# Strassen's seven block products for three and four pairs of k tiles in two down projections

## The chip, the cores and the metric

One core of one Trainium2 chip runs the whole kernel. The metric is device time in microseconds of one execution; shown are the median and the range of three runs. One further execution was profiled, and every row below is from it.

## The reference, cut to what matters

```
def swiglu(x, w_gate, w_up, w_down):
    return (jax.nn.silu(x @ w_gate) * (x @ w_up)) @ w_down
...
        x = layer_norm(alpha * x + 0.5 * swiglu(x, ffn_w_gate[l, 0], ffn_w_up[l, 0], ffn_w_down[l, 0]),
                       ln_g[l, 0], ln_b[l, 0])
        x = layer_norm(alpha * x + hybrid_mixer(x, w_in[l], b_gate[l], diff_lambda[l], diff_subln_g[l],
                                                w_br_moba[l], w_br_diff[l], w_br_sb[l], w_out[l], l),
                       ln_g[l, 1], ln_b[l, 1])
        x = layer_norm(alpha * x + 0.5 * swiglu(x, ffn_w_gate[l, 1], ffn_w_up[l, 1], ffn_w_down[l, 1]),
                       ln_g[l, 2], ln_b[l, 2])
```

There is one layer, 256 tokens, a model width of 1024 and a feed-forward width of 2816. The change lies in the two products with `ffn_w_down`: hidden values of 256 x 2816 times a weight of 2816 x 1024.

## The kernel before

All operands are float32. Each is split into a high part in TensorE's float32r format and the remainder in the same format, and a product is made of three matmuls: high by high, high by low, low by high (`nat_mm`). The hidden values stand transposed in `hT`: per k tile of 128 hidden columns, 256 columns of high parts and 256 of low parts. `xT` holds the transposed input of the gate and up products in the same way.

**Weights.** `Weights` brings every weight as a chunk of 128 x 1024 (or 128 x 768). SyncE issues its transfer into a tile `raw` (5 buffers), ScalarE writes the high half of a tile `w` (9 buffers) or `wx` (3 more, where memory is free), VectorE subtracts and writes the low half. `pump` does this ahead of use as far as buffers allow: with 12 buffers, chunk c is split once chunk c - 12 is used up. So a split's place on ScalarE's and VectorE's queues is where `W.done()` stands in the code. All engines run in order; the program's order is the code's order, except for jobs that `pe.later` puts at a planned TensorE time.

**A feed-forward block.** `ffn` makes 22 hidden tiles (j = 0 to 21) with `trn_mms` and `evac`, and then calls `down`. `down` has 22 k tiles. For all but the last 6 (the tail) it takes one chunk and runs 12 matmuls of 512 columns: two token tiles t, two halves hf of the 1024 columns, three matmuls each, into four PSUM banks `acc`. Then it takes the 6 chunks of the tail and finishes one bank after another: t = 0 hf = 0, t = 0 hf = 1, then t = 1. After each bank `residual` adds it to ALPHA times `x` and makes statistics; `normalise` does the layer norm; `turn_tile`, planned 5.9 us later on TensorE's own count (`T_X`), transposes the normalised `x` with TensorE into `xT`, which the next stage reads. In the first block that next stage is the value projection (`vals`, chunks of 768); the second block ends the kernel.

`down` is also called for the output projection of the mixer, where nothing changes.

Of the kernel before, what the change touches and what calls it, by code (L numbers as in the profile page):

```python
# [21 lines left out]
NF = FF // P  # L22
# [4 lines left out]
ALPHA = 2.0 ** 0.25  # L27
# [3 lines left out]


HL_BUFS = 9
RAW_BUFS = 5
START = 4
WARM = 7

NAT = 2

TAIL_FF, IN_FF = 6, 2  # L40
# [20 lines left out]
class Weights:  # L61
# [34 lines left out]
    def split(self):  # L96
        i = self.n_split
        if i >= self.n_dma:
            self.load()
        _, n, scale = self.chunks[i]  # L100
        raw = self.raw.pop(i)
        w = self.tile(i)
        h, l = w[:, 0, :], w[:, 1, :]
        hv = h.bitcast(F32)
        if scale is None:
            self.nc.scalar.activation(h[:, :n], raw[:, :n], AF.Copy)  # L106
            self.nc.vector.tensor_tensor(l[:, :n], raw[:, :n], hv[:, :n], op=ALU.subtract)  # L107
        else:
            self.nc.scalar.activation(h[:, :n], raw[:, :n], AF.Copy, scale=scale)
            self.nc.vector.scalar_tensor_tensor(  # L110
                l[:, :n], raw[:, :n], scale, hv[:, :n], op0=ALU.mult, op1=ALU.subtract)
        self.hl[i] = (h, l)
        self.n_split += 1

    def pump(self):

# [74 lines left out]
def trunk(ctx: ExitStack, tc: tile.TileContext, start_d, x_d, ln_g, ln_b, gu_d, gun_d, down_d, v_d, qk_d, gate_d,  # L191
# [17 lines left out]
    for f in range(2):  # L209
        nat = NAT if f else 0  # L210
        for b in range(nat):
            chunks += [(gun_d[b, i], 1024, None) for i in range(4)]
        for j in range(2, NF) if f == 0 else range(2 * nat, NF):
            chunks += [(gu_d[f, j, i], 1024, None) for i in range(2)]
        chunks += [(down_d[f, k * P:(k + 1) * P, :], 1024, None) for k in range(NF)]
# [19 lines left out]
    def act_split(dst_h, dst_l, src):  # L235
        nc.scalar.activation(dst_h, src, AF.Copy)  # L236
        nc.vector.tensor_tensor(dst_l, src, dst_h.bitcast(F32), op=ALU.subtract)
# [100 lines left out]
        nc.gpsimd.dma_start(out=b, in_=ln_b[i].partition_broadcast(P))  # L338
        ln_par[i] = (g, b)

    def residual(t, lo, n, ps, st):
        xs = x[:, t, lo:lo + n]
        nc.vector.scalar_tensor_tensor(xs, xs, ALPHA, ps[:, 0:n], op0=ALU.mult, op1=ALU.add)  # L343
        nc.vector.bn_stats(st, xs)

    def normalise(i, t, st, last):
# [60 lines left out]
    def down(lhs, nk, tail, inline, i, last=False):  # L407


        banks = [[acc.tile([P, 512], F32, name="acc") for _ in range(2)] for _ in range(2)]  # L410
        for k in range(nk - tail):
            (h, l), = W.take(1)
            for t in range(2):
                for hf in range(2):
                    nat_mm(banks[t][hf], lhs, k, t, h, l, hf * 512, 512, k == 0,
                           last and t == 1 and hf == 1 and k == nk - tail - 1)
            W.done()
        ws = W.take(tail)

        def part(t, hf, n):  # L420
            k = nk - tail + n
            h, l = ws[n]
            nat_mm(banks[t][hf], lhs, k, t, h, l, hf * 512, 512, k == 0, n == tail - 1)

        for t in range(2):
            st = small.tile([P, 3, 6], F32, name="st")
            left = tail
            if t == 0 or last:
                for n in range(tail):
                    part(t, 0, n)  # L430
                residual(t, 0, 512, banks[t][0], st[:, 0, :])
            if t == 0:
                for n in range(tail):
                    part(t, 1, n)
                residual(t, 512, 512, banks[t][1], st[:, 1, :])
            elif last:
                xs = x[:, t, 512:]
                nc.vector.scalar_tensor_tensor(xs, xs, ALPHA, banks[t][1], op0=ALU.mult, op1=ALU.add)
                for c in range(2):
                    ps = acc.tile([P, 512], F32, name="acc")  # L440
                    for n, (h, l) in enumerate(ws):
                        nat_mm(ps, lhs, nk - tail + n, t, h, l, 512 + c * S, S, n == 0, n == tail - 1)
                    xs = x[:, t, 512 + c * S:512 + (c + 1) * S]
                    nc.vector.tensor_tensor(xs, xs, ps[:, 0:S], op=ALU.add)  # L444
                    nc.vector.bn_stats(st[:, 1 + c, :], xs)  # L445
            else:
                for n in range(tail):
                    part(1, 0, n)
                    part(1, 1, n)
                    if n < inline:  # L450
                        W.done()
                        left -= 1
                for hf in range(2):
                    residual(t, hf * 512, 512, banks[t][hf], st[:, hf, :])
            normalise(i, t, st[:, 0:3 if last and t else 2, :], last)
        if last:
            W.done(left)
        else:
            pe.later(DONE_AT, lambda: W.done(left))


    def ffn(f, i):
        with ExitStack() as es:
            hp = es.enter_context(tc.tile_pool(name="hp", bufs=1))
            tmp = es.enter_context(tc.tile_pool(name="ftmp", bufs=3))
            hT = hp.tile([P, NF, 2 * S], F32R, name="hT")

            def evac(j, banks, free):
                res = []
                for ps in banks:  # L470
                    lo = tmp.tile([P, S], F32, name="lo")
                    nc.scalar.activation(lo, ps[:, S:2 * S], AF.Copy)  # L472
                    v = tmp.tile([P, S], F32, name="gu")
                    nc.vector.tensor_tensor(v, ps[:, 0:S], lo, op=ALU.add)  # L474
                    res.append(v)
                g, u = res
                W.done(free)
                nc.scalar.activation(g, g, AF.Silu)
                nc.vector.scalar_tensor_tensor(u, u, 0.5, g, op0=ALU.mult, op1=ALU.mult)  # L479
                W.done(free)  # L480
                act_split(hT[:, j, 0:S], hT[:, j, S:2 * S], u)

            if f == 0:

                banks = [att.tile([P, 512], F32, name="att") for _ in range(2)]
                for k in range(KT):
                    w, c = first[k // 2], slice((k % 2) * 512, (k % 2) * 512 + 512)
                    for x_lo, w_lo in ((0, 0), (1, 0), (0, 1)):
                        for t in range(2):
                            a = xT[:, k, x_lo * S + t * P:x_lo * S + (t + 1) * P]  # L490
                            pe.mm(banks[t], a, w[:, w_lo, c], k == 0 and x_lo + w_lo == 0, k == KT - 1 and w_lo == 1)
                    if k % 2:
                        W.free(W.held.pop(-k), True)
                units = []
                for t in range(2):
                    pv = banks[t].rearrange("p (j g c) -> p g j c", j=2, g=2)
                    units.append(hidden(tmp, t, pv[:, 0], pv[:, 1]))
                pe.later(N_T, lambda: turn_hidden(hT, 0, units))
            else:
                nat_gate_up(tmp, hT, NAT)  # L500
            for j in range(2 if f == 0 else 2 * NAT, NF):
                ws = W.take(2)
# [5 lines left out]
            down(hT, NF, TAIL_FF, IN_FF, i, last=f == 1)  # L508

    def nat_gate_up(tmp, hT, nat):  # L510
        ws = W.take(4 * nat)
# [459 lines left out]
```

## Time and profile before

| | |
|---|---|
| median of 3 runs | 599.26 us (599.05 to 599.38) |
| the profiled execution's own time | 599.37 us |
| its span, first to last instruction | 597.7 us |
| TensorE busy | 587.9 us |
| VectorE busy | 407.5 us |
| ScalarE busy | 327.0 us |

The span is what the profile shows; the 1.7 us between it and that execution's time lie around it. A busy TensorE is one with a matmul under way, not one at its peak.

### The profile page before, as it was taken

The page shows a single profiled execution, that of the slowest core. Times are in us where ns is not written, and L with a number is a line of the kernel's source. Part 1 is how long each engine was busy: PE and PEld are TensorE (multiplying, and loading weights), DVE is VectorE, ACT ScalarE, POOL GpSimd, SP SyncE. Part 2 cuts the span into 40 slices and gives each one's busy share as a digit, 9 for nine tenths or more (in the row PEclk, how much of TensorE's full clock was granted, in tenths as well). Part 3 has the DMA queues.
Part 4 walks back from the last instruction along what each step waited for, and adds up shares of the span by engine and source line. Part 5 has one row for each costly group of instructions (what it writes and reads, how often), then busy time and mean ns, then how long its engine had stood idle before and what let it go on. Part 6 is the DMA issues. An engine that isn't in the chain of part 4 may idle for free.

```text
span 597.7 us, 8548 instructions
## 1 busy us (share of the span) xinstructions
PE 587.9 (98%) x3150; PEld 505.4 (85%) x3150; DVE 407.5 (68%) x655; ACT 327.0 (55%) x550; POOL 36.2 (6%) x77
## 2 busy tenths in 40 slices
PE   8999999999999999999999999999999999999994
PEld 7888888888888998888888878888898898888884
DVE  6889777674338746597977685889867766764216
ACT  5878656663312758596657654644665665654100
POOL 0610000000001003110001000001000000000002
PEclk9999999999999999999999999999999999999998
DMA  8998755666442676354547447356965566564001
GB/s 308 326 392 303 255 183 180 206 185 227 140 127 63 209 249 239 115 176 149 171 141 243 144 163 255 107 172 225 316 240 180 178 205 184 181 214 165 1 0 70
DMA packets 32537, 113.34 MB, mean 190 GB/s; under 512 B 3680, under 2 KB 4448, under 8 KB 32496
## 3 DMA queue, kind: packets, MB, share of 16 engines
q1 hardware_dynamic: 30816, 106.97, 53.9%
q0 software_dynamic: 1680, 5.83, 2.9%
q8 instruction: 24, 0.39, 0.3%
q14 instruction: 17, 0.14, 0.1%
HBM read 111.74 MB, written 1.05 MB: 189 GB/s over the span
## 4 chain that ended last, share of the span: by engine, by line
PE 98%; DMA 1%; DVE 0%; POOLq 0%; SPq 0%; POOL 0%; ACT 0%; issue 0%; DVEq 0%
PE acc L182 91%; PE att L182 5%; PE att L186 2%; DMA sraw<-start 1%; DVE x L361 0%; POOLq L965 0%; SPq L246 0%; POOL rs L351 0%; ACT w L272 0%; DVE st L445 0%; DVE x L444 0%; DVEq L965 0%; DVE mv L350 0%
## 5 line engine op out<-in xcount | busy, mean ns | idle before, releaser
L107 DVE TENSOR_TENSOR w<-raw,w 128x1024 fp32r<-128x1024 f32 (+1 forms) x166 | 197.7, 1207 | 62.4 <-ACT w L106 61.8
L182 PE MATMUL acc<-xT,w 128*128 128x512 f32 (+1 forms) x1264 | 226.4, 337 | 0.0
L182 PEld LDWEIGHTS acc<-xT,w 128*128 128x128 f32 x1264 | 196.2, 190 | 26.7 <-issue 1.0
L106 ACT ACTIVATE w<-raw 128x1024 fp32r<-128x1024 f32 (+1 forms) x166 | 170.2, 1041 | 68.9 <-PE acc L182 60.3
L182 PE MATMUL acc<-w,xT 128*128 128x512 f32 (+1 forms) x576 | 128.2, 379 | 0.0
L182 PEld LDWEIGHTS acc<-w,xT 128*128 128x128 f32 x576 | 105.5, 188 | 18.6 <-issue 1.0
L182 PE MATMUL acc<-w,hT 128*128 128x512 f32 (+1 forms) x408 | 93.1, 383 | 0.0
L182 PEld LDWEIGHTS acc<-w,hT 128*128 128x128 f32 x408 | 75.2, 188 | 15.0
L472 ACT ACTIVATE lo<-acc 128x256 f32<-128x256 f32 x76 | 28.7, 383 | 57.5 <-PE acc L182 57.5
L474 DVE TENSOR_TENSOR gu<-acc,lo 128x256 f32<-128x256 f32 x76 | 31.5, 422 | 34.8 <-ACT lo L472 34.6
L182 PE MATMUL acc<-xT,wx 128*128 128x256 f32 (+1 forms) x240 | 46.1, 337 | 0.0
L107 DVE TENSOR_TENSOR wx<-raw,wx 128x1024 fp32r<-128x1024 f32 (+1 forms) x30 | 36.3, 1213 | 13.2 <-ACT wx L106 13.0
L182 PEld LDWEIGHTS acc<-xT,wx 128*128 128x128 f32 x240 | 37.5, 190 | 4.4
L106 ACT ACTIVATE wx<-raw 128x1024 fp32r<-128x1024 f32 (+1 forms) x30 | 31.3, 1047 | 12.1 <-PE acc L182 10.2
L182 PE MATMUL acc<-wx,hT 128*128 128x512 f32 (+1 forms) x138 | 32.8, 380 | 0.0
L182 PEld LDWEIGHTS acc<-wx,hT 128*128 128x128 f32 x138 | 25.2, 188 | 4.9
L351 POOL TENSOR_SCALAR rs<-mv 128x1 f32<-128x1 f32 x6 | 4.7, 778 | 405.4 <-DVE mv L350 405.4
L343 DVE SCALAR_TENSOR_TENSOR x<-x,acc 128x512 f32<-128x512 f32 x11 | 7.5, 682 | 27.2 <-PE acc L182 27.2
L182 PE MATMUL acc<-w,oT 128*128 128x512 f32 x108 | 25.7, 393 | 0.0
L182 PEld LDWEIGHTS acc<-w,oT 128*128 128x128 f32 x108 | 20.1, 188 | 4.4 <-issue 0.3
L236 ACT ACTIVATE hT<-gu 128x256 fp32r<-128x256 f32 x38 | 15.8, 415 | 11.6 <-DVE gu L479 11.6
L479 DVE SCALAR_TENSOR_TENSOR gu<-gu 128x256 f32<-128x256 f32 x38 | 15.9, 419 | 0.0
(146 smaller groups left out, 401.3 us busy)
## 6 DMA issues: line engine op xcount, KB each, us to landing
raw<-gu SPq DMA_DIRECT2D x76, 512.0 KB, 4.8
raw<-down SPq DMA_DIRECT2D x44, 512.0 KB, 4.1
raw<-gates SPq DMA_DIRECT2D x24, 512.0 KB, 4.4
raw<-qk SPq DMA_DIRECT2D x18, 512.0 KB, 4.6
raw<-v SPq DMA_DIRECT2D x12, 384.0 KB, 3.1
raw<-w_out SPq DMA_DIRECT2D x8, 512.0 KB, 4.4
raw<-gun SPq DMA_DIRECT2D x8, 512.0 KB, 4.3
sraw<-start SPq DMA_DIRECT2D x7, 384.0 KB, 6.3
```

The costliest lines, as they stand in the source:

```text
L106: self.nc.scalar.activation(h[:, :n], raw[:, :n], AF.Copy)
L107: self.nc.vector.tensor_tensor(l[:, :n], raw[:, :n], hv[:, :n], op=ALU.subtract)
L182: self.nc.tensor.matmul(out, lhsT=lhsT, rhs=rhs, start=start, stop=stop, **kw)
L186: self.nc.tensor.transpose(out, in_, ident)
L236: nc.scalar.activation(dst_h, src, AF.Copy)
L343: nc.vector.scalar_tensor_tensor(xs, xs, ALPHA, ps[:, 0:n], op0=ALU.mult, op1=ALU.add)
L351: nc.gpsimd.tensor_scalar(rs, mv[:, 1:2], EPS, None, op0=ALU.add)
L472: nc.scalar.activation(lo, ps[:, S:2 * S], AF.Copy)
L474: nc.vector.tensor_tensor(v, ps[:, 0:S], lo, op=ALU.add)
L479: nc.vector.scalar_tensor_tensor(u, u, 0.5, g, op0=ALU.mult, op1=ALU.mult)
```

## The change

For the k tiles just ahead of the tail, two k tiles ka and kb are taken together: 3 pairs in the first feed-forward block, 4 in the second. Over a pair the product is a 2 x 2 by 2 x 2 product of blocks: rows are the token tiles t, columns the halves hf, the inner index ka and kb. Instead of 8 block products (24 matmuls of 512 columns) it makes 7 (21 matmuls) by Strassen's algorithm in Winograd's form.

Four operands are sums of hidden blocks (`sums_T`, at the head of `down` for all pairs; written to `xT`, which is free by then, after a high/low split). Four are sums of weight blocks: a pair's weights become four chunks named "first" to "fourth", made by `split_sums` from the two `raw` tiles. Four products go to PSUM banks of their own (`p1`, `p5`, `p6`, `p7`, pool `att`), three straight into `acc`. After the last pair, ScalarE copies `p1` and eight VectorE instructions add the four banks to `x`, with a scratch tile `u`. `residual` then scales by 1.0. The tile `sums` has one buffer that `sums_T`, "third", "fourth" and `u` share; `raw` goes from 5 buffers to 4.

```diff
-RAW_BUFS = 5
+RAW_BUFS = 4
...
+PAIRS = (3, 4)
...
+    def split_cols(self, src, h, l, cs):
+        self.nc.scalar.activation(h[:, cs], src, AF.Copy)
+        self.nc.vector.tensor_tensor(l[:, cs], src, h[:, cs].bitcast(F32), op=ALU.subtract)
+
+    def split_sums(self, which, raw, h, l):
...
+        sub, lo, hi = self.nc.vector.tensor_tensor, slice(0, 512), slice(512, 1024)
+        if which == "first":
+            self.upper = raw
+            self.split_cols(raw[:, lo], h, l, lo)
+            sub(raw[:, lo], raw[:, hi], raw[:, lo], op=ALU.subtract)
+            self.split_cols(raw[:, lo], h, l, hi)
+        elif which == "third":
+            self.sums = self.raw_pool.tile([P, 1024], F32, name="sums", bufs=1)
+            sub(self.sums.rearrange("p (i c) -> p i c", i=2),
+                self.lower[:, hi].unsqueeze(1).to_broadcast([P, 2, 512]),
+                self.upper.rearrange("p (i c) -> p i c", i=2), op=ALU.subtract)
+            self.split_cols(self.sums, h, l, slice(0, 1024))
+        else:
+            sub(self.lower[:, lo], self.lower[:, lo], self.sums[:, lo], op=ALU.subtract)
+            self.split_cols(self.lower[:, lo], h, l, lo)
...
+    def sums_T(lhs, ka, kb, i):
...
+        t = rawp.tile([P, 1024], F32, name="sums", bufs=1)
+        tt = nc.vector.tensor_tensor
+        for n, k in enumerate((ka, kb)):
+            hl = lhs[:, k, :].bitcast(F32)
+            tt(t[:, n * S:(n + 1) * S], hl[:, 0:S], hl[:, S:2 * S], op=ALU.add)
+        a, c, b, d, s1, s2, s3, s4 = (t[:, n * P:(n + 1) * P] for n in range(8))
+        tt(s1, c, d, op=ALU.add)
+        tt(s2, s1, a, op=ALU.subtract)
+        tt(s3, a, c, op=ALU.subtract)
+        tt(s4, b, s2, op=ALU.subtract)
+        place = xT[:, 2 * i:2 * i + 2, :].rearrange("p k (n c) -> p (k n) c", c=2 * P)
+        act_split(place[:, :, 0:P], place[:, :, P:2 * P], t[:, 512:1024].rearrange("p (n c) -> p n c", c=P))
+        return [(place[:, n, 0:P], place[:, n, P:2 * P]) for n in range(4)]
...
+        std = nk - tail - 2 * pairs
+        s_ops = [sums_T(lhs, std + 2 * n, std + 2 * n + 1, n) for n in range(pairs)]
+        for k in range(std):
...
+                for m, prods in enumerate((((p1, plain(ka, 0)), (p5, s1)),
+                                           ((banks[0][0], plain(kb, 0)), (banks[0][1], s4)),
+                                           ((p6, s2), (p7, s3)),
+                                           ((banks[1][0], plain(kb, 1)),))):
+                    for half, (ps, (a, al)) in enumerate(prods):
...
+                        pe.mm(ps, a, h, first, False)
+                        pe.mm(ps, a, l, False, False)
+                        pe.mm(ps, al, h, False, end)
+                    W.done()
+            u = rawp.tile([P, 1024], F32, name="sums", bufs=1)[:, 0:512]
...
+            nc.scalar.activation(u, p1, AF.Copy)
+            add(0, 0, p1, ALPHA)
+            nc.vector.tensor_tensor(u, u, p6, op=ALU.add)
+            add(0, 1, u, ALPHA)
+            add(0, 1, p5, 1.0)
+            nc.vector.tensor_tensor(u, u, p7, op=ALU.add)
+            add(1, 0, u, ALPHA)
+            add(1, 1, u, ALPHA)
+            add(1, 1, p5, 1.0)
         ws = W.take(tail)
```

What this does to VectorE's order is seen at two places. The first is the start of the first `down`, from the end of hidden tile 21 on (L237 before and L278 after write `hT`; L107 before and L116 after are the plain split of a chunk). Before:

```order
L107 TENSOR_TENSOR w<-raw,w 128x1024
L237 TENSOR_TENSOR hT<-gu,hT 128x256
L107 TENSOR_TENSOR w<-raw,w 128x1024 x3
L107 TENSOR_TENSOR wx<-raw,wx 128x1024
L107 TENSOR_TENSOR w<-raw,w 128x1024 x2
```

After, the operands of the first pair (L455 to L460 are the sums of `sums_T`, the last row is their split):

```order
L116 TENSOR_TENSOR w<-raw,w 128x1024
L278 TENSOR_TENSOR hT<-gu,hT 128x256
L455 TENSOR_TENSOR sums<-hT 128x256 x2
L457 TENSOR_TENSOR sums<-sums 128x128
L458 TENSOR_TENSOR sums<-sums 128x128
L459 TENSOR_TENSOR sums<-sums 128x128
L460 TENSOR_TENSOR sums<-sums 128x128
L278 TENSOR_TENSOR xT<-sums,xT 128x4x128
```

The last six of these rows follow twice more, for the other pairs, and then come the weights. The rows down to the first L126 of 512 columns are "third" and "fourth" of the first pair, whose "first" and "second" stand before the sums; then come the second pair's four chunks (L126 is a low half in `split_cols`; L136, L140 and L145 are the weight sums of "first", "third" and "fourth"):

```order
L140 TENSOR_TENSOR sums<-raw 128x1024
L126 TENSOR_TENSOR w<-sums,w 128x1024
L145 TENSOR_TENSOR raw<-raw,sums 128x512
L126 TENSOR_TENSOR w<-raw,w 128x512 x2
L136 TENSOR_TENSOR raw<-raw 128x512
L126 TENSOR_TENSOR w<-raw,w 128x512
L116 TENSOR_TENSOR wx<-raw,wx 128x1024
L140 TENSOR_TENSOR sums<-raw 128x1024
L126 TENSOR_TENSOR w<-sums,w 128x1024
L145 TENSOR_TENSOR raw<-raw,sums 128x512
L126 TENSOR_TENSOR w<-raw,w 128x512
```

Where two splits stood for two k tiles, eight VectorE instructions stand per pair, and five of them read what a ScalarE instruction has just written. The second place is the end of the first `down`'s splits (768 columns are chunks of the value projection). Before:

```order
L107 TENSOR_TENSOR w<-raw,w 128x768 x5
L107 TENSOR_TENSOR wx<-raw,wx 128x768
L343 SCALAR_TENSOR_TENSOR x<-x,acc 128x512
L344 BN_STATS st<-x 128x6
L343 SCALAR_TENSOR_TENSOR x<-x,acc 128x512
```

After:

```order
L116 TENSOR_TENSOR w<-raw,w 128x768 x2
L116 TENSOR_TENSOR wx<-raw,wx 128x768
L505 SCALAR_TENSOR_TENSOR x<-x,att 128x512
L509 TENSOR_TENSOR sums<-sums,att 128x512
L505 SCALAR_TENSOR_TENSOR x<-x,sums 128x512
L505 SCALAR_TENSOR_TENSOR x<-x,att 128x512
L512 TENSOR_TENSOR sums<-sums,att 128x512
L505 SCALAR_TENSOR_TENSOR x<-x,sums 128x512 x2
L505 SCALAR_TENSOR_TENSOR x<-x,att 128x512
L384 SCALAR_TENSOR_TENSOR x<-x,acc 128x512
L385 BN_STATS st<-x 128x6
```

The eight additions of the product banks stand between the splits and the first residual, and the splits of six value chunks stand ahead of them.

## Rows read from the trace of the kernel before

**Rows 1.** The page: busy time by engine, and the chain that ended last.

```profile
PE 587.9 (98%) x3150; PEld 505.4 (85%) x3150; DVE 407.5 (68%) x655; ACT 327.0 (55%) x550; POOL 36.2 (6%) x77
...
PE 98%; DMA 1%; DVE 0%; POOLq 0%; SPq 0%; POOL 0%; ACT 0%; issue 0%; DVEq 0%
```

**Rows 2.** Stretches: us; busy PE, PEld, DVE, ACT, POOL; clock; DMA.

```profile
128.20:155.40 27.20, 27.20 (x122) 22.52 (x121) 14.46 (x14) 12.44 (x14) 0.00 (x0) 1.00 0.63 199
...
551.40:573.10 21.70, 21.70 (x97) 17.98 (x96) 3.67 (x3) 3.18 (x3) 0.00 (x0) 1.00 0.00 1
```

**Rows 3.** Timeline of PE, first down: start, length, line, tiles, count.

```profile
128.16 8.32 PE L182 MATMUL acc<-w,hT 128*128 128x512 f32 x36
136.32 2.88 PE L182 MATMUL acc<-wx,hT 128*128 128x512 f32 x12
...
186.19 1.03 PE L186 MATMUL att<-ident,x 128*128 128x128 f32 x8
...
188.90 3.31 PE L182 MATMUL acc<-w,xT 128*128 128x384 f32 x18
```

**Rows 4.** Timeline of DVE, first down; in brackets the idle time before and its releaser.

```profile
130.93 0.42 DVE L479 SCALAR_TENSOR_TENSOR gu<-gu 128x256 f32<-128x256 f32 x1
131.26 1.22 DVE L107 TENSOR_TENSOR w<-raw,w 128x1024 fp32r<-128x1024 f32 x1
132.40 0.42 DVE L237 TENSOR_TENSOR hT<-gu,hT 128x256 fp32r<-128x256 f32 x1
...
134.89 1.23 DVE L107 TENSOR_TENSOR w<-raw,w 128x1024 fp32r<-128x1024 f32 x1 [0.89 <-ACT w L106]
...
175.96 0.69 DVE L343 SCALAR_TENSOR_TENSOR x<-x,acc 128x512 f32<-128x512 f32 x1 [2.24 <-PE acc L182]
176.69 0.69 DVE L344 BATCH_NORM_STATS2 st<-x 128x6 f32<-128x512 f32 x1
...
181.49 0.21 DVE L350 BATCH_NORM_AGGREGATE mv<-st 128x2 f32<-128x12 f32 x1
...
184.71 0.75 DVE L361 SCALAR_TENSOR_TENSOR x<-x,rs,ln_b 128x512 f32<-128x512 f32 x1
```

**Rows 5.** Timeline of ACT, first down.

```profile
133.80 1.06 ACT L106 ACTIVATE w<-raw 128x1024 fp32r<-128x1024 f32 x1 [1.05 <-PE acc L182]
```

**Rows 6.** Groups of DVE and ACT by form: count, busy us, mean ns, idle before.

```profile
L889 DVE TENSOR_TENSOR G<-G 128x512 f32<-128x512 f32 x8 | 5.5, 692 | 0.3
L710 DVE TENSOR_TENSOR o<-att,rsm 128x256 f32<-128x256 f32 x3 | 1.3, 425 | 1.0 <-PE att L182 1.0
L613 DVE CUSTOM_DVE_ANT_0 e<-att,base 128x128 f32<-128x128 f32 x12 | 3.4, 287 | 0.0
...
L236 ACT ACTIVATE w<-sraw 128x512 fp32r<-128x512 f32 x5 | 3.1, 616 | 0.0
```

**Rows 7.** Timeline of PE, second down: its start and its last matmuls.

```profile
529.60 13.76 PE L182 MATMUL acc<-w,hT 128*128 128x512 f32 x60
...
588.59 1.24 PE L182 MATMUL acc<-w,hT 128*128 128x256 f32 x9
```

**Rows 8.** Timeline of DVE, second down.

```profile
533.84 0.42 DVE L237 TENSOR_TENSOR hT<-gu,hT 128x256 fp32r<-128x256 f32 x1
...
577.40 0.69 DVE L343 SCALAR_TENSOR_TENSOR x<-x,acc 128x512 f32<-128x512 f32 x1 [18.03 <-PE acc L182]
...
590.79 0.24 DVE L350 BATCH_NORM_AGGREGATE mv<-st 128x2 f32<-128x18 f32 x1
```

**Rows 9.** The same view after the last matmul; the clock is third from last.

```profile
590.00:590.50 0.50, 0.00 (x0) 0.00 (x0) 0.47 (x2) 0.00 (x0) 0.00 (x0) 1.00 0.00 0
...
592.00:592.50 0.50, 0.00 (x0) 0.00 (x0) 0.47 (x1) 0.00 (x0) 0.50 (x1) 0.50 0.00 0
```

**Rows 10.** First matmuls of the kernel: ns min/median/max, first and last start.

```profile
L182 PE MATMUL att<-w,xT x48: 389/389/767, 4.2 to 16.4; 128*128 128x512 f32 x48
L253 PE MATMUL att<-warm x14: 421/421/583, 1.1 to 4.0; 128*128 128x128 f32 x14
```

More of the change, by code (lines that the diff above doesn't have):

```diff
@@ L78, in load @@
         src, n, _ = self.chunks[i]
+        if src is None:
+            self.n_dma += 1
+            return
         t = self.raw_pool.tile([P, 1024], F32, name="raw")
@@ L100, in split @@
         _, n, scale = self.chunks[i]
-        raw = self.raw.pop(i)
+        raw = self.raw.pop(i, None)
         w = self.tile(i)
@@ L104, in split @@
         hv = h.bitcast(F32)
-        if scale is None:
+        if scale in ("first", "third", "fourth"):
+            self.split_sums(scale, raw, h, l)
+        elif scale in (None, "second"):
+            if scale:
+                self.lower = raw
             self.nc.scalar.activation(h[:, :n], raw[:, :n], AF.Copy)
@@ L214, in trunk @@
             chunks += [(gu_d[f, j, i], 1024, None) for i in range(2)]
-        chunks += [(down_d[f, k * P:(k + 1) * P, :], 1024, None) for k in range(NF)]
+        for k in range(NF):
+            src = down_d[f, k * P:(k + 1) * P, :]
+            n = k - (NF - TAIL_FF - 2 * PAIRS[f])
+            if not 0 <= n < 2 * PAIRS[f]:
+                chunks += [(src, 1024, None)]
+            elif n % 2 == 0:
+                chunks += [(src, 1024, "first")]
+            else:
+                chunks += [(src, 1024, "second"), (None, 1024, "third"), (None, 512, "fourth")]
         if f == 0:
@@ L339, in ln_load, with residual @@
         ln_par[i] = (g, b)
-    def residual(t, lo, n, ps, st):
+    def residual(t, lo, n, ps, st, scale):
         xs = x[:, t, lo:lo + n]
-        nc.vector.scalar_tensor_tensor(xs, xs, ALPHA, ps[:, 0:n], op0=ALU.mult, op1=ALU.add)
+        nc.vector.scalar_tensor_tensor(xs, xs, scale, ps[:, 0:n], op0=ALU.mult, op1=ALU.add)
         nc.vector.bn_stats(st, xs)
@@ L405, in trn_mms, with down @@
                               skip_group_check=True)
-    def down(lhs, nk, tail, inline, i, last=False):
+    def sums_T(lhs, ka, kb, i):
[12 more added lines that the diff above has]
+        return [(place[:, n, 0:P], place[:, n, P:2 * P]) for n in range(4)]
+    def down(lhs, nk, tail, inline, i, last=False, pairs=0):
         banks = [[acc.tile([P, 512], F32, name="acc") for _ in range(2)] for _ in range(2)]
-        for k in range(nk - tail):
+        std = nk - tail - 2 * pairs
+        s_ops = [sums_T(lhs, std + 2 * n, std + 2 * n + 1, n) for n in range(pairs)]
+        for k in range(std):
             (h, l), = W.take(1)
@@ L415, in down, with plain, add @@
                     nat_mm(banks[t][hf], lhs, k, t, h, l, hf * 512, 512, k == 0,
-                           last and t == 1 and hf == 1 and k == nk - tail - 1)
+                           last and t == 1 and hf == 1 and k == std - 1)
             W.done()
+        scale = ALPHA
+        if pairs:
+            scale = 1.0
+            p1, p5, p6, p7 = (att.tile([P, 512], F32, name="att") for _ in range(4))
+            for n in range(pairs):
+                ka, kb = std + 2 * n, std + 2 * n + 1
+                (s1, s2, s3, s4), ws = s_ops[n], W.take(4)
+                def plain(k, t):
+                    return lhs[:, k, t * P:(t + 1) * P], lhs[:, k, S + t * P:S + (t + 1) * P]
+                for m, prods in enumerate((((p1, plain(ka, 0)), (p5, s1)),
[3 more added lines that the diff above has]
+                    for half, (ps, (a, al)) in enumerate(prods):
+                        first, end = (n == 0, n == pairs - 1) if m in (0, 2) else (False, False)
+                        h, l = (w[:, half * 512:(half + 1) * 512] for w in ws[m])
+                        pe.mm(ps, a, h, first, False)
[3 more added lines that the diff above has]
+            u = rawp.tile([P, 1024], F32, name="sums", bufs=1)[:, 0:512]
+            def add(t, hf, src, scale):
+                xs = x[:, t, hf * 512:(hf + 1) * 512]
+                nc.vector.scalar_tensor_tensor(xs, xs, scale, src, op0=ALU.mult, op1=ALU.add)
+            nc.scalar.activation(u, p1, AF.Copy)
[7 more added lines that the diff above has]
+            add(1, 1, p5, 1.0)
         ws = W.take(tail)
@@ L430, in down @@
                     part(t, 0, n)
-                residual(t, 0, 512, banks[t][0], st[:, 0, :])
+                residual(t, 0, 512, banks[t][0], st[:, 0, :], scale)
             if t == 0:
@@ L434, in down @@
                     part(t, 1, n)
-                residual(t, 512, 512, banks[t][1], st[:, 1, :])
+                residual(t, 512, 512, banks[t][1], st[:, 1, :], scale)
             elif last:
                 xs = x[:, t, 512:]
-                nc.vector.scalar_tensor_tensor(xs, xs, ALPHA, banks[t][1], op0=ALU.mult, op1=ALU.add)
+                nc.vector.scalar_tensor_tensor(xs, xs, scale, banks[t][1], op0=ALU.mult, op1=ALU.add)
                 for c in range(2):
@@ L453, in down @@
                 for hf in range(2):
-                    residual(t, hf * 512, 512, banks[t][hf], st[:, hf, :])
+                    residual(t, hf * 512, 512, banks[t][hf], st[:, hf, :], scale)
             normalise(i, t, st[:, 0:3 if last and t else 2, :], last)
@@ L507, in ffn @@
                     ln_load(i)
-            down(hT, NF, TAIL_FF, IN_FF, i, last=f == 1)
+            down(hT, NF, TAIL_FF, IN_FF, i, last=f == 1, pairs=PAIRS[f])
     def nat_gate_up(tmp, hT, nat):
```

## The prediction

> **What bounds the kernel now.** I read the page first: TensorE is busy for 587.9 of 597.7 us, and the chain that ended last is TensorE for 98% of the span [rows 1]. So time is won only where matmuls go, and lost wherever TensorE is made to wait. Then I read the stretches of the two down products [rows 2]: in the first 27 us of the first one TensorE is busy without a gap at a granted clock of 1.00, and VectorE for about half (14.46 of 27.20 us); in the pair stretch of the second down VectorE is busy for only 3.67 of 21.70 us. That looks like room. But room on average is not what a queue in order needs, so I read the timelines of TensorE, VectorE and ScalarE one instruction at a time [rows 3 to 5, 7, 8]. In them the reader is to see two things. A split is made once a buffer comes free (ScalarE waits for TensorE, VectorE for ScalarE), so the splits run 12 chunks, or 12 x 2.72 = 33 us of matmuls, ahead. And ScalarE's instruction and VectorE's stand strictly one after the other: 133.80 + 1.06 = 134.86, and VectorE starts at 134.89 [rows 4, 5].
>
> **What it removes.** 36 matmuls lie between 128.16 and 136.32 us [rows 3]: 0.2267 us each. Three fewer per pair, seven pairs: 21 x 0.2267 = 4.76 us (2.04 in the first block, 2.72 in the second). TensorE needs 21 x 0.2267 = 4.76 us for one pair.
>
> **Prices on the other engines.** VectorE, 1024 columns: 1.22 us alone, 1.14 in a row (131.26 to 132.40); 256 columns: 0.42 alone, 0.33 in a row [rows 4]; 512 columns in SBUF: 0.69 [rows 6], so 0.61 in a row by the same overlap; a dependent instruction starts 0.04 after its source ends (175.96 + 0.69 to 176.69) [rows 4]. No plain 128-column operation is in the rows; the nearest takes 0.287 [rows 6]. An operand that is broadcast costs no more: 0.425 for 256 columns [rows 6], so "third" is priced as a plain 1024. In place costs nothing extra (L889, 0.692). ScalarE: 1.06 for 1024 [rows 5]; 0.62 for 512 [rows 6], of which my chains use 0.60, so that a pair is too short by 0.04 us at most.
>
> In the Trainium skill, VectorE: DVE Perf Modes, Terms, an instruction cannot issue before the pipeline of the one ahead has emptied. The rows overlap by 0.08 us, so the measurement decides; by the page some 33 independent steps of the second block would add 33 x 0.08 = 2.6 us.
>
> **One pair's weights** are then, in VectorE's order and with its waits: low half of "fourth" of the pair before 0.61; "first": low half 0.73, weight sum 0.73, ScalarE's high half 0.64, then ScalarE's 1.06 for "second", begun behind it, which leaves 0.96 to its low half; low half of "second" 1.26; sum of "third" 1.26, ScalarE 1.10, low half 1.14; sum of "fourth" 0.73, ScalarE 0.64. Sum 9.80 us, of which 6.47 are work (5 x 0.61 + 3 x 1.14). TensorE eats a pair in 4.76. **One pair's hidden sums** are 0.33 + 0.46 + 0.32 + 0.21 + 0.21 + 0.33, ScalarE 0.64, split 0.73: 3.24 us, and the one buffer `sums` lets no two overlap. So per pair VectorE is held for 13 us in place of two splits, 2.3. The lead must pay.
>
> **First down (3 pairs).** In hidden tile 21, "first" replaces a plain split: by the same prices its last write starts at 133.84, not 132.40 [rows 4]. Sums for three pairs: to 143.8. Rest of pair one (1.26 + 1.10 + 1.14 + 0.73 + 0.64): 148.7. Two pairs: 168.3. ScalarE's first tail chunk holds the next split until 169.2; six tail splits at 1.14: 176.1. TensorE has meanwhile run 10 plain tiles (to 155.36) and the pairs (to 169.6), just in time; but its first tail bank wants all six chunks within 4.1 us, by 173.7, and ends at 176.7: 3 us late. Next in VectorE's queue stand six value splits (0.96 - 0.08 each by the nearest rows, 5.3): 181.4; then the eight additions, 5.4: 186.7. Only now comes the first residual, which ran at 175.96 before. From it to the end of the first layer norm: statistics and second residual 2.8, then 4.0 as before (181.49 to 184.71 + 0.75) [rows 4]: 193.5. TensorE's transposes stood at 186.19, 64 matmuls into the tail [rows 3]; 18 of these end at 176.7, the other 46 at 187.1, and there TensorE waits, the second four until 193.5. With these four (0.44) and the 8 matmuls left (1.81) the stage ends at 195.8, not 188.90: **+6.9 us**, the 2.04 saved already in it. What hid such work before, the 18 us of tail matmuls, is used up.
>
> **Clock.** TensorE's granted clock reads 1.00 at 590.0 and 0.50 at 592.0, the last matmul having ended at 589.8 [rows 7, 9]. The wait of 5 to 6 us is longer. After the kernel's start the matmuls from 1.1 us on ran slow, the slowest 767 ns, until past 4.2 us [rows 10]. If the return takes as long here, some 3.7 us run at half speed: **+1.8 us** (bounds 0 and 3.7).
>
> **Second down (4 pairs).** Pair one's "first", "third" and "fourth" replace three plain splits in hidden tiles 20 and 21; the last write moves from 533.84 [rows 8] to 536.6. Sums of four pairs: to 549.9. Three pairs at 9.80: the last low half starts at 578.5. Six tail splits: 586.4. TensorE wants its third pair at 561 and from there on follows VectorE with waits of about 1 us; its first tail bank ends at 586.9, and the 54 matmuls' worth left (18 + 18 + 36 of 256 columns) at 599.2, where it was 588.59 + 1.24 = 589.8 [rows 7]: +9.3. VectorE adds the product banks until 591.7 (first residual was 577.40 [rows 8]), and norms the first token tile until 598.0, so that the second tile's residuals, behind it in the queue, end later still: the last aggregate starts at 601.8, not 590.79 [rows 8]: **+11.0 us**.
>
> `raw` with 4 buffers: a pair's transfers are as many as before, and the lead is 33 us: 0, at most one chunk's ScalarE time, 1.1.
>
> **Sum.** 599.37 (the profiled execution, 0.11 over the median) + 6.9 + 1.8 + 11.0 = 619.1; **619.0** against the median.
>
> **Rivals.**
> *The lead covers it (faster).* If ScalarE's turns were hidden behind other VectorE work, a pair would cost 6.47, saving 3.33 per pair: with those of the sums some 10 us in the first down, where 6.9 + 2.0 = 8.9 have to go for the whole gain, and 13 in the second, where it is 11.0 + 2.7 = 13.7. That is the point from which it decides: all gaps gone. Then little but the matmuls counts: 599.26 - 4.76 + 0.7 = 595.2. For it: VectorE's 68% [rows 1]. Against: the order, in which each next instruction needs the ScalarE result that is waited for. Chance 0.06.
> *Half of the gaps are hidden* (ScalarE faster from SBUF, pairs overlapping): 5 us less in the first, 6.5 in the second: 607.5. Chance 0.14.
> *The clock falls in the second down too.* There TensorE works 4.76 of 9.80 us. At 1.2 GHz a pair takes 9.5 us, still under VectorE's pace, but the first tail bank takes 18 x 0.453 = 8.2 instead of 7.3, and the first 3.7 us after it lose 1.8: about 622; with no return before the end, 12 us more, 632. For: the fall in rows 9. Against: no wait there is longer than 1.3 us. The Trainium skill, TensorE: Matmul & The Clock Gate, HAM oscillation, has frequent small idle gaps between matmul groups throttle the clock over and over, and so bears out this rival; no row of before has such gaps. Chance 0.18.
> *My forecast*, one clock fall and both queues as laid out: 0.60. Nothing measurable (losses and gains cancel): 0.02.
>
> **Range and chances.** 0.2% is what a measurement tells from no change. Holding 8 in 10 takes in the half-hidden case and the milder clock case: 607 to 628. Faster 0.06, same 0.02, slower 0.92.
>
> **What would show it.** Right: 20 us per two pairs between plain splits on VectorE; TensorE's idle before the transposes about 5 us, named as a wait for `x`; second down with waits of about 1 us for `w` from the third pair on; the first residual of the second block 14 us later in its stage. Wrong: VectorE's period per pair near 6.5; no idle before the transposes; TensorE at 0.5 through the second down; or a TensorE wait in the first 60 us, which would be `raw`.

## The result, and the profile after

The changed kernel takes 628.11 us (median of 6 runs, 627.23 to 629.65), against 599.32 us for the kernel before in the same comparison (6 runs): a ratio of 1.0478, 95% interval 1.0467 to 1.0489. It is 28.8 us slower; forecast were 19.7, and 628.11 lies 0.1 us above the upper end of the range.

| us from the span's start | before | after | longer by |
|---|---|---|---|
| first `down` starts | 128.16 | 128.12 | 0.0 |
| value projection starts (end of that stage) | 188.90 | 203.59 | 14.7 |
| second `down` starts | 529.60 | 544.47 | 14.9 |
| start of the last aggregate, from the start of the second `down` | 61.19 | 74.89 | 13.7 |
| span | 597.7 | 626.2 | 28.5 |

The page: busy time, and the chain that ended last.

```profile
PE 601.1 (96%) x3129; PEld 507.0 (81%) x3129; DVE 464.9 (74%) x762; ACT 343.7 (55%) x580; POOL 36.1 (6%) x77
...
PE 76%; DVE 12%; ACT 5%; DMA 3%; issue 2%; POOL 0%; POOLq 0%; SPq 0%; ACTq 0%; DVEq 0%
```

21 matmuls fewer, and yet TensorE is only 76% of the chain, where it was 98% [rows 1]. VectorE is busy for 57 us more and has 12% of the chain, ScalarE 5% and transfers 3%, where the three had 0, 0 and 1%. The timelines show who waits for whom.

VectorE, first `down` (L140 the sum of "third", L126 the low halves of "first", "third" and "fourth", L116 plain splits, L505 additions, L402 the norm's last step):

```profile
143.90 1.23 DVE L140 TENSOR_TENSOR sums<-raw 128x1024 f32<-128x1024 f32 x1
...
148.90 1.29 DVE L126 TENSOR_TENSOR w<-raw,w 128x512 fp32r<-128x512 f32 x2 [0.76 <-ACT w L125]
...
158.70 0.69 DVE L126 TENSOR_TENSOR w<-raw,w 128x512 fp32r<-128x512 f32 x1 [0.76 <-ACT w L125]
...
168.56 0.69 DVE L126 TENSOR_TENSOR wx<-raw,wx 128x512 fp32r<-128x512 f32 x1 [0.78 <-ACT wx L125]
169.51 3.50 DVE L116 TENSOR_TENSOR w<-raw,w 128x1024 fp32r<-128x1024 f32 x3 [0.26 <-ACT w L115]
...
176.56 1.23 DVE L116 TENSOR_TENSOR w<-raw,w 128x1024 fp32r<-128x1024 f32 x1 [1.56 <-ACT w L115]
...
187.19 0.68 DVE L505 SCALAR_TENSOR_TENSOR x<-x,att 128x512 f32<-128x512 f32 x1
...
198.46 0.75 DVE L402 SCALAR_TENSOR_TENSOR x<-x,rs,ln_b 128x512 f32<-128x512 f32 x1
```

Up to 169.51 this is the prediction's ledger: the sums end at 143.90 (forecast 143.8), the low half of "fourth" comes at 148.90 (148.7), the next two 9.80 and 9.86 us behind, and the first tail split starts at 169.51 (169.2). Then it leaves the ledger: the additions start at 187.19, not 181.4, and before them no residual can be formed, which ran at 175.96 in the kernel before [rows 4]. ScalarE's timeline says why; the brackets name what each of its copies waited for.

```profile
168.43 2.94 ACT L115 ACTIVATE w<-raw 128x1024 fp32r<-128x1024 f32 x3
172.69 1.06 ACT L115 ACTIVATE w<-raw 128x1024 fp32r<-128x1024 f32 x1 [1.31 <-DMA raw<-down]
175.47 1.06 ACT L115 ACTIVATE w<-raw 128x1024 fp32r<-128x1024 f32 x1 [1.72 <-DMA raw<-down]
...
181.17 0.84 ACT L115 ACTIVATE wx<-raw 128x768 fp32r<-128x768 f32 x1 [1.21 <-DMA raw<-v]
183.19 0.85 ACT L115 ACTIVATE w<-raw 128x768 fp32r<-128x768 f32 x1 [1.17 <-DMA raw<-v]
```

Three tail chunks lie ready in `raw`; the three behind them do not, nor do five of the six value chunks. The view by source of the issues of these transfers between 126 and 184 us shows when SyncE sent them (duration of an issue in ns, then the first and the last start). Before (this view is not among the rows above):

```profile
L80 SPq DMA_DIRECT2D raw<-v x11: 327/328/328, 147.0 to 173.7; - x11
L80 SPq DMA_DIRECT2D raw<-down x8: 327/328/328, 126.9 to 144.3; - x8
```

After:

```profile
L85 SPq DMA_DIRECT2D raw<-down x9: 327/328/328, 126.9 to 171.9; - x9
L85 SPq DMA_DIRECT2D raw<-v x7: 327/328/328, 173.0 to 183.0; - x7
...
DMA to landing us min/median/max: 3.3/3.9/4.7
```

The last `down` transfer is issued at 171.9, not at 144.3, and lands 3.3 to 4.7 us later. SyncE's own waits, in the view of waits from 120 to 200 us, name what it stood behind:

```profile
SPq L85 <- DVE sums L140: 27.9, 3, 17.9
SPq L85 <- DVE w L116: 10.0, 9, 2.4
SPq L85 <- DVE w L126: 8.0, 2, 4.0
```

A `raw` tile of a pair comes free only when "third" (L140) or "fourth" has read it, and SyncE, in order, waits for that. The longest of the three waits for L140, 17.9 us, covers the hidden sums, during which VectorE frees no tile. In the kernel before SyncE waits for tiles too, but for plain splits, and at most 12.2 us; there no ScalarE copy of the tail waits for a transfer:

```profile
SPq L80 <- DVE w L107: 49.3, 16, 12.2
```

TensorE, first `down`:

```profile
170.79 0.96 PE L215 MATMUL acc<-w,hT 128*128 128x512 f32 x3 [0.52 <-DVE w L116]
...
175.06 0.73 PE L215 MATMUL acc<-w,hT 128*128 128x512 f32 x2 [0.75 <-DVE w L116]
176.58 0.78 PE L215 MATMUL acc<-w,hT 128*128 128x512 f32 x1 [0.80 <-ACT w L115]
...
197.81 1.11 PE L219 MATMUL att<-ident,x 128*128 128x128 f32 x4 [5.51 <-DVE x L402]
...
200.03 1.20 PE L215 MATMUL acc<-w,hT 128*128 128x512 f32 x2
201.03 2.76 PE L215 MATMUL acc<-wx,hT 128*128 128x512 f32 x6
203.59 2.43 PE L215 MATMUL acc<-w,xT 128*128 128x384 f32 x12
```

In the tail TensorE waits chunk by chunk, then comes the long wait before the transposes. The 8 matmuls behind it take 203.59 - 200.03 = 3.56 us, not 8 x 0.2267 = 1.81.

TensorE and VectorE, second `down`:

```profile
578.75 0.73 PE L215 MATMUL acc<-wx,hT 128*128 128x512 f32 x2 [0.51 <-DVE wx L116]
...
581.04 0.50 PE L215 MATMUL att<-wx,xT 128*128 128x512 f32 x1 [0.86 <-ACT wx L125]
```

```profile
583.61 1.29 DVE L126 TENSOR_TENSOR w<-raw,w 128x512 fp32r<-128x512 f32 x2 [0.76 <-ACT w L125]
...
593.45 0.69 DVE L126 TENSOR_TENSOR wx<-raw,wx 128x512 fp32r<-128x512 f32 x1 [0.78 <-ACT wx L125]
...
602.55 1.22 DVE L116 TENSOR_TENSOR wx<-raw,wx 128x1024 fp32r<-128x1024 f32 x1
...
619.36 0.24 DVE L391 BATCH_NORM_AGGREGATE mv<-st 128x2 f32<-128x18 f32 x1
```

The period is 9.84 us here, and from the third pair on TensorE follows VectorE with waits under 1 us. The last tail split starts at 602.55: 6 splits at 1.14 from 594.39 on would have put it at 600.1. ScalarE waits for transfers there too (1.32, 1.55 and 0.21 us).

The clock, in stretches (same columns as [rows 2]):

```profile
176.70:183.30 6.60, 6.12 (x14) 4.32 (x15) 5.09 (x5) 3.60 (x5) 0.00 (x0) 0.50 0.79 244
...
197.20:203.80 6.60, 5.65 (x17) 4.48 (x18) 6.12 (x9) 1.20 (x2) 0.00 (x0) 0.50 0.35 118
582.90:586.10 3.20, 3.20 (x9) 2.44 (x8) 1.98 (x3) 1.59 (x3) 0.00 (x0) 0.50 0.26 58
587.00:592.90 5.90, 3.67 (x12) 2.20 (x13) 4.21 (x5) 1.42 (x3) 0.00 (x0) 1.00 0.29 95
593.10:596.30 3.20, 3.20 (x8) 1.68 (x8) 2.60 (x3) 3.16 (x4) 0.00 (x0) 0.50 0.33 99
603.40:606.60 3.20, 2.98 (x8) 2.22 (x8) 3.13 (x6) 0.00 (x0) 0.00 (x0) 0.50 0.00 0
```

The third column from the right is the granted clock; 0.50 is the lower level, 1.2 GHz. It reads 0.50 twice in the first `down`, the second time after the long wait, as forecast, and three times in the second.

### The profile page after: what moved, and what is told of

Same layout as the page of the kernel before. It is cut to its first block, busy times and chain, and to the rows that moved or that the text cites. A ratio compares the mean times of both kernels' runs of the same rounds, so it can differ in the third digit from the quotient of the medians.

```text
span 626.2 us, 8655 instructions
## 1 busy us (share of the span) xinstructions
PE 601.1 (96%) x3129; PEld 507.0 (81%) x3129; DVE 464.9 (74%) x762; ACT 343.7 (55%) x580; POOL 36.1 (6%) x77
## 4 chain that ended last, share of the span: by engine, by line
PE 76%; DVE 12%; ACT 5%; DMA 3%; issue 2%; POOL 0%; POOLq 0%; SPq 0%; ACTq 0%; DVEq 0%
PE acc L215 70%; PE att L215 4%; DVE w L126 2%; ACT w L125 2%; PE att L219 2%; DVE w L116 2%; DMA raw<-v 1%; DVE sums L140 1%; ACT w L115 1%; DMA raw<-down 1%; DVE sums L455 1%; DVE raw L136 1%; ACT xT L277 1%; DMA sraw<-start 1%; DVE xT L278 1%
## 5 line engine op out<-in xcount | busy, mean ns | idle before, releaser
L116 DVE TENSOR_TENSOR w<-raw,w 128x1024 fp32r<-128x1024 f32 (+1 forms) x160 | 190.5, 1208 | 49.6 <-ACT w L115 48.6
L115 ACT ACTIVATE w<-raw 128x1024 fp32r<-128x1024 f32 (+1 forms) x160 | 164.0, 1042 | 48.9 <-PE acc L215 15.9
L215 PE MATMUL acc<-w,xT 128*128 128x512 f32 (+1 forms) x579 | 130.8, 380 | 0.0
L215 PE MATMUL acc<-w,hT 128*128 128x512 f32 (+1 forms) x318 | 81.5, 402 | 5.7 <-DVE w L116 4.3
L215 PEld LDWEIGHTS acc<-w,hT 128*128 128x128 f32 x318 | 60.4, 199 | 23.4 <-DVE w L116 8.7
L116 DVE TENSOR_TENSOR wx<-raw,wx 128x1024 fp32r<-128x1024 f32 (+1 forms) x29 | 34.9, 1205 | 7.9 <-ACT wx L115 7.8
L215 PE MATMUL acc<-wx,hT 128*128 128x512 f32 (+1 forms) x102 | 29.5, 422 | 0.7 <-DVE wx L116 0.7
L215 PE MATMUL att<-w,xT 128*128 128x512 f32 x102 | 27.8, 409 | 2.2 <-DVE w L126 1.1
L215 PEld LDWEIGHTS att<-w,xT 128*128 128x128 f32 x102 | 19.4, 194 | 8.4 <-DVE w L126 2.2
L215 PEld LDWEIGHTS acc<-wx,hT 128*128 128x128 f32 x102 | 20.2, 206 | 7.0 <-DVE wx L116 2.0
```

Of the source, the lines that this page charges most:

```text
L215: self.nc.tensor.matmul(out, lhsT=lhsT, rhs=rhs, start=start, stop=stop, **kw)
```

## The experiments

My theory after reading this: a pair's chain on VectorE and ScalarE (9.80 us) costs what the prediction says, and the rest of the loss is `raw`, whose tiles come free late. Rivals: the loss lies in VectorE's added work as such; the clock makes it; `raw` with 4 buffers costs something everywhere.

**`raw` with 4 buffers, without the change.** The kernel before with `RAW_BUFS = 4`.

> The kernel before with 4 raw buffers instead of 5 and nothing else. My theory says that raw buffers cost time only where pairs hold two of them; without pairs the splits stand 25 us ahead and nothing changes: 599.3, within 0.5 us. The rival, that one raw buffer less slows the stream of weights everywhere, gives several us more, up to the 8 us that the ledger of my prediction lacks: 602 to 608.

Measured: 600.63 us, ratio 1.0018 (1.0007 to 1.0030); a little over the 0.5 us expected. The profiled execution is the fastest of the ten (599.35 us); its span is 597.6 us, as before, with the same milestones, so it shows no place where the buffer is missed. With plain splits the fifth buffer is worth at most 0.3%.

**One block at a time.** `PAIRS = (3, 0)` and `(0, 4)`.

> The change with 3 pairs in the first down and none in the second. In the profile after, the value projection starts 14.7 us later and the second down 14.9 us later than before. If the two downs lose independently, 599.3 + 14.8 = 614.1. If part of the second loss comes from the first (a lead not recovered), less than 13.7 is left for the second run of this pair, and the two losses don't add to 28.8.

> The change with no pairs in the first down and 4 in the second. By the profile after, the second down alone is 28.6 - 14.9 = 13.7 us longer: 613.0. With e2 the two losses should add up to 28.8 us within 1 us.

Measured: 614.04 us (1.0231, 1.0214 to 1.0249) and 614.48 us (1.0250, 1.0223 to 1.0278). The losses, 14.4 and 14.9 us against 599.62, add up to 29.3 where both together lose 28.8: the two blocks lose apart from one another, the first 14.4 where 6.9 + 1.8 stood, the second 14.9 where 11.0 stood. In the profile of (0, 4) the second `down` itself is 14.0 us longer; 1.4 us come before it, where little but `raw` differs from the kernel before.

**A fifth buffer.** Both blocks, with memory for it taken from the hidden tiles' scratch pool.

```diff
-RAW_BUFS = 4
+RAW_BUFS = 5
-            self.sums = self.raw_pool.tile([P, 1024], F32, name="sums", bufs=1)
+            self.sums = self.sums_pool.tile([P, 1024], F32, name="sums")
...
-            tmp = es.enter_context(tc.tile_pool(name="ftmp", bufs=3))
+            tmp = es.enter_context(tc.tile_pool(name="ftmp", bufs=2))
+            W.sums_pool = es.enter_context(tc.tile_pool(name="sump", bufs=1))
```

> The change with 5 raw buffers and the sums tile in the feed-forward block's own memory; its scratch tiles go from 3 buffers to 2 to make room. My theory: the waits of ScalarE for transfers in the tails (5.8 us until the last value split, 2.5 us until the last tail split of the second down) come from the two raw buffers that a pair holds. With a fifth most of them go: 622 to 624; all of them gone would be 628.1 - 8.3 = 619.8. The rival, that these transfers are slow for another reason, leaves 628.

Measured: 623.28 us (1.0388, 1.0371 to 1.0405), 4.8 us less than the change. In the profiled executions it is 4.1: 2.1 in the first part (second `down` starts at 542.34) and 1.95 in the second. Waits for transfers are left: 1.12 and 0.55 us for value chunks, 1.50 and 0.30 for tail chunks in the first `down`. So the missing buffer costs 4 to 5 us, with the smaller scratch pool in it, and five don't do either.

**No sums of weights.** "first", "third" and "fourth" are plain splits of the upper, upper and lower block; L136, L140 and L145 are left out.

```diff
-            self.split_cols(raw[:, lo], h, l, lo)
-            sub(raw[:, lo], raw[:, hi], raw[:, lo], op=ALU.subtract)
-            self.split_cols(raw[:, lo], h, l, hi)
+            self.split_cols(raw, h, l, slice(0, 1024))
...
-            self.split_cols(self.sums, h, l, slice(0, 1024))
+            self.split_cols(self.upper, h, l, slice(0, 1024))
...
-            sub(self.lower[:, lo], self.lower[:, lo], self.sums[:, lo], op=ALU.subtract)
```

> The change (3 and 4 pairs, 4 raw buffers) without the three weight sums of a pair: first, third and fourth are plain splits of the pair's raw tiles, all matmuls, hidden sums and additions stay. It leaves out that part of the computation. A pair then costs VectorE 3 x 1.14 + 0.61 = 4.0 us, with no turn of ScalarE inside, in place of 9.8. My theory: the chain through the weight sums is what runs TensorE dry; without it both downs keep their saving, 599.3 - 4.8 = 594.5, up to 3 us more where raw buffers still hold up the tail. The rival, that the additions of the product banks or the extra PSUM work hold the layer norm up by themselves, leaves 605 or more.

Measured: 599.79 us (1.0009, 0.9998 to 1.0021): nearly the whole loss is gone, but it is a miss, for 597.5 at most was expected. In the profile (of the fastest of ten executions, 598.51 us) the second `down` takes 58.47 us, 2.72 less than before: all of its saved matmuls. The sums of hidden blocks, the three extra half tiles of each pair and the eight additions are still in it; so it is the weight sums, with their turns between the engines and all that is late through them, that cost the second block 13.7 + 2.7 us. The first still loses 1.9 us until the second starts, with a wait before the transposes of 1.85 us: the additions stand behind tail and value chunks for whose transfers ScalarE waits up to 1.59 us.

**Fewer pairs.** `PAIRS = (2, 2)`.

> The change with 2 pairs in each down, everything else as in the change. Saved matmuls: 12 x 0.2267 = 2.7 us. VectorE's chain ends 13 us earlier in the first down (one pair of 9.8 and one of 3.24 less), so the additions are done by 177 us and the first layer norm by 184, about when the transposes want it (184.8). If the loss is only VectorE running out of its lead: 596.6 to 597.5, faster than before. If each pair costs its share of the loss (28.8 us over 7 pairs, 4.1 each), it is 616.

Measured: 602.75 us (1.0045, 1.0030 to 1.0060), a miss. The second block behaves (59.83 us, 1.36 less: all of two pairs' saving). The first loses 5.5 us until the second starts. ScalarE's timeline shows the reason: it waits for transfers after only two pairs, and the additions stand behind the value chunks.

```profile
162.56 1.06 ACT L115 ACTIVATE w<-raw 128x1024 fp32r<-128x1024 f32 x1 [1.40 <-DMA raw<-down]
165.13 1.06 ACT L115 ACTIVATE w<-raw 128x1024 fp32r<-128x1024 f32 x1 [1.50 <-DMA raw<-down]
...
170.71 0.85 ACT L115 ACTIVATE w<-raw 128x768 fp32r<-128x768 f32 x1 [1.23 <-DMA raw<-v]
172.81 0.85 ACT L115 ACTIVATE w<-raw 128x768 fp32r<-128x768 f32 x1 [1.25 <-DMA raw<-v]
```

**A pair's four buffers filled in one go**, with five `raw` buffers: VectorE gets its instructions in an order in which ScalarE's copies lie beside other VectorE work, where the change waits out each one. In the first two runs the sum of "third" is formed from the unmodified upper block, so it is another sum of weights than the change's (not "the same arithmetic", as the first expectation has it), with as many instructions of the same size.

```diff
+        act(h1[:, lo], upper[:, lo], AF.Copy)
+        act(h2, lower, AF.Copy)
+        low(l1[:, lo], upper[:, lo], h1[:, lo])
+        sub(upper[:, lo], upper[:, hi], upper[:, lo], op=ALU.subtract)
+        sub(sums.rearrange("p (i c) -> p i c", i=2), lower[:, hi].unsqueeze(1).to_broadcast([P, 2, 512]),
+            upper.rearrange("p (i c) -> p i c", i=2), op=ALU.subtract)
+        act(h1[:, hi], upper[:, lo], AF.Copy)
+        act(h3, sums, AF.Copy)
+        low(l2, lower, h2)
+        sub(lower[:, lo], lower[:, lo], sums[:, lo], op=ALU.subtract)
+        act(h4[:, lo], lower[:, lo], AF.Copy)
+        low(l1[:, hi], upper[:, lo], h1[:, hi])
+        low(l3, sums, h3)
+        low(l4[:, lo], lower[:, lo], h4[:, lo])
```

(This is the order of the last two; in the first two L140's sum stands ahead of everything.)

> As e4 (3 and 4 pairs, 5 raw buffers), with the eight VectorE and five ScalarE instructions of a pair in another order: third's sum first, and every low half at least one VectorE instruction behind the ScalarE instruction that it reads. The same arithmetic. If ScalarE's turns inside the chain are a third of a pair's 9.8 us, the period falls to 6.5 us and the time from 623.3 to 606 to 610. If VectorE's work alone were the limit, it stays at 623.

> The kernel of e7 with 2 pairs in the first down and 3 in the second. Saved matmuls: 15 x 0.2267 = 3.4 us. VectorE ends its splits at about 161 us in the first down, ahead of TensorE, and at about 573 in the second, where the first tail bank ends at 575. Theory: nothing is lost, 595.9 to 597. If the additions delay the layer norms all the same: 599 to 602.

> Pairs (2, 3), 5 raw buffers, a pair's four buffers filled in one go as in e8, but the sum of the third is formed from the upper block as the change has it (behind the weight sum of the first). The number of instructions is that of e8; VectorE has one more wait on ScalarE per pair, at its start (0.73 us). If the gain of e8 came from grouping and from fewer pairs: first down -0.5 to +1.5, second -2.0 (its three pairs' whole saving), 595.5 to 598. If the order inside the pair matters as much as the grouping: a loss of 2 us or more in the first down, over 599.

> The same corrected pair with pairs (3, 4). If the pair's period is what counts (about 7.3 us grouped, 9.8 ungrouped): 606 to 611, first down +3 to +5, second +4 to +6. If the first wait of a pair undoes the grouping: 615 or more.

Measured, in this order: 607.01 us (1.0123, 1.0109 to 1.0137), 596.24 us (0.9944, 0.9931 to 0.9957), 597.02 us (0.9957, 0.9944 to 0.9969), 607.42 us (1.0132, 1.0117 to 1.0148). Where the sum of "third" stands within a pair matters little: 0.8 and 0.4 us. VectorE in the last of the four, second `down` (L165 is the sum of "third"):

```profile
555.75 1.23 DVE L165 TENSOR_TENSOR sums<-raw 128x1024 f32<-128x1024 f32 x1
...
562.54 1.23 DVE L165 TENSOR_TENSOR sums<-raw 128x1024 f32<-128x1024 f32 x1
...
569.33 1.22 DVE L165 TENSOR_TENSOR sums<-raw 128x1024 f32<-128x1024 f32 x1
```

A pair takes 6.79 us, not 9.80, and no VectorE wait lies in it: almost the 6.47 us of pure work. TensorE still wants one every 4.76, so that four pairs run the lead out (the second `down` is 4.3 us longer than before) and three do not: the second `down` of the third run, (2, 3), takes 59.14 us, 2.05 less than before, all of three pairs' saving (2.04). Its first `down` brings nothing (the second starts at 529.96, 0.4 later than before), since TensorE waits before the transposes:

```profile
185.01 0.66 PE L255 MATMUL att<-ident,x 128*128 128x128 f32 x4 [0.34 <-DVE x L438]
186.46 0.66 PE L255 MATMUL att<-ident,x 128*128 128x128 f32 x4 [0.80 <-DVE x L438]
```

This version, with the change's own sums, is 0.4% faster than the kernel before: a small gain, but its slowest run, 597.68, lies below the fastest of the kernel before, 599.08.

**The same pairs, not grouped.** `PAIRS = (2, 3)` and five `raw` buffers, split as the change does.

> Pairs (2, 3) with 5 raw buffers and the pairs as the change splits them, not grouped: what of e9 is the number of pairs. One pair less takes 3.24 + 9.80 - 2 x 1.14 = 10.8 us from VectorE: second down 11.75 - 10.8 = about +1, first down +3 to +4 (5.5 in e6, less the 2 that the fifth buffer gave): 603 to 605. If the number of pairs alone made the gain: 596 to 597, as e8.

Measured: 603.27 us (1.0057, 1.0044 to 1.0071). Against the grouped kernel of the same pairs, 597.02, grouping is worth 6.2 us; fewer pairs alone don't make the gain. The total is as expected, its parts are not: the first block loses 0.7 us (3 to 4 expected) and the second 3.1 (1 expected). So the fifth buffer gave the two-pair first block 4.8 us, not 2.

**No late transfers.** The change as it is, with 18 transfers left out: the six tail chunks of each `down` and the first six value chunks are split from a tile that already lies in SBUF.

```diff
-        if src is None:
+        if src is None or scale == "resident":
...
+            elif scale:
+                raw = self.resident
...
-                chunks += [(src, 1024, None)]
+                chunks += [(src, 1024, "resident" if n >= 0 else None)]
...
+        W.resident = g
```

> The change as it is (3 and 4 pairs, 4 raw buffers), but 18 chunks aren't transferred: the six tail chunks of each down and the first six value chunks are split from a tile that already lies in SBUF (the layer norm's weights), with the same ScalarE and VectorE instructions. It leaves out 18 transfers, and so every wait for a transfer behind the pairs. If these waits are what the prediction priced at 0: its own terms are left, 6.9 + 1.8 in the first down and 11.0 in the second, 618 to 621. If the excess over the prediction lies in ScalarE's and VectorE's own work or in the clock: 625 to 628. Half of each: 622 to 624.

Measured: 620.05 us (1.0342, 1.0317 to 1.0367). VectorE and TensorE in the first `down`, and VectorE's last aggregate:

```profile
169.31 5.77 DVE L118 TENSOR_TENSOR w<-ln_g,w 128x1024 fp32r<-128x1024 f32 x5 [0.25 <-ACT w L117]
...
181.34 0.68 DVE L508 SCALAR_TENSOR_TENSOR x<-x,att 128x512 f32<-128x512 f32 x1
...
192.60 0.75 DVE L405 SCALAR_TENSOR_TENSOR x<-x,rs,ln_b 128x512 f32<-128x512 f32 x1
...
611.27 0.24 DVE L394 BATCH_NORM_AGGREGATE mv<-st 128x2 f32<-128x18 f32 x1
```

```profile
191.96 0.76 PE L221 MATMUL att<-ident,x 128*128 128x128 f32 x4 [4.54 <-DVE x L405]
193.41 1.12 PE L221 MATMUL att<-ident,x 128*128 128x128 f32 x4 [0.69 <-DVE x L405]
...
197.74 2.92 PE L217 MATMUL acc<-w,xT 128*128 128x384 f32 x12
```

With no transfer to wait for, the prediction's terms are what is left. The additions start at 181.34 (forecast 181.4), the norm ends at 193.35 (193.5), the stage ends at 197.74 (195.8 + 1.8 = 197.6), and the last aggregate comes 72.16 us after its `down` starts, 10.97 later than before (11.0). The late transfers, and the waits and falls of the clock that they bring with them, cost the change 628.11 - 620.05 = 8.1 us, 5.4 until the second `down` starts (at 539.11 here) and 2.7 in it.

## Why the prediction was right, and where it was not

**Right: the direction and the mechanism.** VectorE's and ScalarE's alternating steps make a pair 9.80 us where TensorE takes 4.76: 9.80 and 9.86 are measured in the first block. Independent VectorE steps overlap by 0.08 us in the trace after too (131.44 + 0.69 = 132.13, the next starts at 132.05), as the prices have it. Without the weight sums the second block has its whole gain; with the gaps closed by grouping, a pair takes 6.79 us and 15.9 us of the loss go with it (623.28 to 607.42, both with five buffers). Whether part of that comes from `raw` tiles that grouping frees earlier was not measured apart; ScalarE still waits for transfers there (0.46 and 1.85 us in the second tail).

**Right: the two places and their terms.** In the first block the wait before the transposes, in the second VectorE's pace to the end. 6.9 + 1.8 and 11.0 were forecast; 8.84 and 10.97 are measured once transfers are out of the way. Before the transposes TensorE waits 4.54 + 0.69 us in that run, "about 5" by the prediction, and the first residual of the second block comes 14.2 us later in its stage (14 forecast; 16.7 in the change). The clock's term fits at the end of the stage: 3.56 - 1.81 = 1.75 us. Its reasoning does not. The 3.7 us at half speed don't follow from [rows 10] (1.1 to past 4.2 us), and the stretch after the long wait reads 0.50 for 6.60 us. It reaches into the value projection: without late transfers, its first 12 matmuls take 2.76 us, where 12 such take 2.08 at clock 1.00, and the second `down` starts 9.5 us later, not 8.7. That the term fits is in part luck.

**Mis-sized: "`raw` with 4 buffers: 0, at most one chunk's ScalarE time, 1.1".** The missing buffer cost 4 to 5 us and the late transfers in all 8.1, where the sum had 0. The reason given was the error: the lead of 33 us is that of the splits over their use by TensorE. Transfers lead the splits only by the tiles of `raw`; a pair holds two of the four until "third" and "fourth" are made, and as soon as splits follow each other in 1.14 us, each transfer of 3.3 to 4.7 us is seen. The prediction would have looked for it in the first 60 us, but the first `down` starts no later than before (128.12); the place is the end of each `down`. In the kernel before, 4 buffers do; the change itself made them too few, and five give back 4.8 of the 8.1.

**The rival of the clock.** The Trainium skill, TensorE: Matmul & The Clock Gate, A second HAM failure mode (the section behind the one that the prediction names), tells of a bf16 kernel that cycles through PSUM banks, where frequent small idle gaps between groups of matmuls make the clock fall and rise again and again. The trace after agrees, with waits for `w` as the gaps: 0.50 in three stretches of the second `down`, with waits of 0.2 to 0.9 us around them. But it did not decide: with the clock fallen only once (at 578.1) and no transfers, the second block still loses 10.97 us, so VectorE's pace sets it there. What share of the 8.1 us the falls have that come with the late transfers was not measured apart.

**The other rivals.** "Half of the gaps are hidden" (607.5) is not this kernel. The 607.42 of the grouped one meets its number by accident: grouping closes nine tenths of a pair's gaps (9.80 - 6.79 = 3.01 of 3.33 us), and waits for transfers, which that rival did not have, take part of it back. "The lead covers it" holds for three grouped pairs in the second block alone.

## What to carry to other kernels

A saving on the bound engine is paid from queues in order on the others: count the producers' period per unit with every hand-off between engines in it, against the consumer's, and how many units the lead carries. Steps that alternate between two engines should be issued for several tiles at once, so that each engine works while the other does. And a source tile that is read more often is held longer: a prefetch depth that was enough for one reader has to be counted anew, at the place where consumption is fastest, not on average.

## What was not expected of the hardware

The granted clock fell to 0.50 in the second `down` though no wait of TensorE there is longer than 0.9 us; between 587.0 and 592.9, where TensorE is busy for only 3.67 of 5.90 us, it reads 1.00, and the fall comes just behind. With two pairs in the first `down` it fell in one kernel and not in the other: at (2, 2) with four buffers, after waits of 2.24 and 0.71 us, the 8 matmuls after the transposes took 193.27 - 189.71 = 3.56 us; at (2, 3) with five, not grouped, after a wait of 0.79 us, 189.15 - 187.21 = 1.94.
